# An encoder layer on one core: where the row factors' diagonal is kept, how the turns of two preparing tasks are spaced, and how much dense work stands between the steps of two mLSTMs

## The chip, the cores and the metric

The kernel runs on one core of one Trainium2 chip. The metric is the device time in microseconds (us) of one execution. The kernel before takes 2711.15 us, the median of 3 runs (2709.81 to 2713.0). Engines are named as in the profile: PE is TensorE's matmul, PEld its weight load, DVE is VectorE, ACT ScalarE, POOL GpSimd and SP SyncE, whose queue issues nearly all transfers.

## What is computed

One layer is applied to two sequences, s = 0 with 1024 tokens and s = 1 with 2048, both with 16 learned meta tokens ahead of them. Cut to what matters:

```
xn   = rmsnorm(h) * g_pre
proj = xn @ w_in + b_in                       # 1024 -> 6672 columns, in ten parts
ya   = (neighbourhood_attention(na_q, na_k, na_v) * silu(na_z)) @ w_a
yb   = (mlstm_both_directions(ml_qk, ml_v, ml_g, ml_o) * silu(ml_z)) @ w_b
y    = (sigmoid(ga) * ya + sigmoid(gb) * yb) @ w_out
out  = h + rmsnorm(y) * g_post                # the meta tokens are dropped
```

The mLSTM has 4 heads of 128 columns and works in chunks. Everything is float32; a dense product is made of three matmuls on parts of the operands (high times high, high times low, low times high).

## The kernel before

The work is one **dense** stream and one **sparse** stream, both Python generators. The dense stream (`dense`, `group`, `fm_half`, `tm_unit`, `sgates`, `final`) holds the big products: the projection of blocks of 1024 tokens by groups of columns in the order of `PLAN`, then the output products. The sparse stream (`sparse`) is, in this order, the mLSTM of s = 0 (the short one), the attention of s = 0, the mLSTM of s = 1 (the long one) and the attention of s = 1. A sparse step begins only when the dense columns that it reads are done.

`run` (L2077) weaves the two. A sparse generator yields a number after each step, and `run` then advances the dense stream until as much dense work, in the generators' own estimate (`C512` = 0.235 for a matmul of 512 columns), has been emitted. The numbers are written at the top: `A_D` = 1.63 for a step of an mLSTM's states, `A_A` = 1.79 for a step of its outputs, `A_G` = 1.3 for its gates. PE's instructions stay in the order in which they are emitted. Those of DVE, ACT and of SP's queue are ordered by a scheduler from its own estimates, so a load or a small operation can stand far ahead of the place where the code has it; each engine then works through its list strictly in order, and so does SP's queue.

An mLSTM (`ml`, L1431) runs `ml_states` and then `ml_outputs` for each of 4 heads. `ml_states` has three steps for each chunk of 256 tokens: DVE makes `kf` (L1500), PE transposes it (L1536), and products with the weighted values follow (L202 to L204 into `sm`). The loads of a chunk (`raw`, L1414, and `va`, L1473) are emitted about one chunk ahead. `ml_outputs` has six steps for a block of 256 tokens; its products with `q` and `kh` (L1665, L1666) are the scores.

`build_half` (L466) makes the normalised input of 512 tokens for the dense stream, in steps that are spread among its matmuls. For the four halves of s = 1 it loads four tiles of token rows (`xr`, L398), squares them (L355), computes the four row factors by Newton steps (L161 to L166), and `rdiag` (L362) writes the diagonal matrices of the factors (L367 on ACT, L369 on DVE). `rrows` (L372) multiplies ones with that diagonal on PE (L375), so that each row factor stands in every partition, and copies the product into `rx` (L376). The transposed input comes in four loads (`xt`, L405) into the same ring of four buffers as the token rows, tag `xr`. DVE multiplies each of them by gain and row factors (L524), and ACT and DVE split them into high and low parts (L531, L532). The diagonal is written into the last token tile, so that buffer is free for a load only after PE has read the diagonal, and the fourth `xt` load is emitted behind `rrows`.

The **output ring** is a ring of four buffers named `st` of 528 columns, in which `fm_evac` (L669) puts each finished projection unit before its store (two buffers for a unit of a gated column).

Three **side tasks** are advanced from `beside` (L547), one step in every so many turns of the dense stream: `tprep` (L626) forms sums and differences of the two halves of a 1024-token block for a product scheme with fewer multiplications and stores them (L629, L661, L665; for s = 0 also a copy of the scaled input, L648 to L651), `nprep` and `wprep` (L565) do the like for weights, from which the operands named `q6..` to `q13..` come (L569, L595).

Of the kernel before, what the change touches and what calls it, by code (L numbers as in the profile page):

```python
# [10 lines left out]
F32 = mybir.dt.float32  # L11
# [7 lines left out]
P = 128  # L19
# [112 lines left out]

NBW = 4
C512, C256 = 0.235, 0.12
A_N, A_D, A_A, A_G = (1.08, 0.93), 1.63, 1.79, 1.3


class K:
# [327 lines left out]
    def build_half(self, s, t0, res):  # L466

        nc, wp = self.nc, self.wp
        if (s, t0) in self.xkept:
            assert not self.xput  # L470
            yield
            yield "scaled"
            x = []
            for name, part in zip(("xh", "xl"), self.xkept[s, t0]):
                x.append(wp.tile([P, KT, HALF], F32R, name=name, bufs=2))
                for k in range(0, KT, 4):
                    nc.sync.dma_start(x[-1][:, k:k + 4, :512].bitcast(F32), part[:, k:k + 4, :])
                yield
            res.append(tuple(x))
            return  # L480
        if s == 0:
            xts = self.xnext
            self.xnext = None
            while self.rwait:
                yield "wait"
            self.early = False
            yield "scaled"
            g = self.gpre
            p = self.psum("sm", [P, 512])
            nc.tensor.matmul(p[:, :KT], self.ident, g, start=True, stop=True)  # L490
            g = self.cp.tile([P, KT], F32, name="gx")
            nc.vector.tensor_copy(g, p[:, :KT])
            x, r = self.xparts(), []
            for e in range(4):
                self.xsplit(x, xts[e], e, 0, g)
                self.wflush(2)
                yield
            res.append(tuple(x))
            yield from self.rsum(self.toks, r)
            nc.vector.tensor_copy(self.rc[:, 4:8], r[0])  # L500
            dg = self.rdiag(r[0], self.toks[0][0])

            def rows():
                self.rrows(dg, self.rr[:, 1], "sm")
                self.xp.close()
                self.wside = self.wprep()
                self.sides.append([self.wside, 3])
            self.rwait[s, t0] = rows
        else:
            bp = self.bp  # L510
            toks, r = self.tokens(s, t0, range(4), bp, 4), []
            yield
            yield from self.rsum(toks, r)
            dg = self.rdiag(r[0], toks[3][0])
            xts = [self.xtload(s, t0, e, bp, 4) for e in range(3)]
            yield
            rr = bp.tile([P, 512], F32, name="rx", tag="thT", bufs=1)
            self.rrows(dg, rr, "pj")
            self.loose = False
            xts.append(self.xtload(s, t0, 3, bp, 4))  # L520
            yield
            for k in range(KT):
                v = xts[k // 2][:, k % 2]
                nc.vector.scalar_tensor_tensor(v, v, self.gpre[:, k:k + 1], rr, op0=ALU.mult, op1=ALU.mult)  # L524
                if k % 2:
                    yield
            yield "scaled"
            x = self.xparts()
            for e in range(4):
                h = x[0][:, 2 * e:2 * e + 2, :512]  # L530
                nc.scalar.activation(h, xts[e], AF.Copy)  # L531
                nc.vector.tensor_tensor(x[1][:, 2 * e:2 * e + 2, :512], xts[e], h.bitcast(F32), op=ALU.subtract)  # L532
                yield
            res.append(tuple(x))
            self.loose = True
            self.xkeep(s, t0, x)
# [28 lines left out]
    def wprep(self):  # L565

        nc = self.nc
        unit = {k: j for j, k in enumerate(_weight_units())}
        sub = lambda o, a, b: nc.vector.tensor_tensor(o, a, b, op=ALU.subtract)  # L569
        self.pq = ExitStack()  # L570
        pool = self.pq.enter_context(self.tc.tile_pool(name="pq", bufs=1, side="right", reuse_waits="tile"))
        for p in range(6, 14):
            if p == 10:
                [x for x in self.sides if x[0] is self.wside][0][1] = 4
            raw = pool.tile([P, 2, 2, 512], F32, name="pr", bufs=1)
            for f in range(2):
                nc.sync.dma_start(raw[:, f].rearrange("p a c -> p (a c)"), self.i["wu"][unit["i", PAIRS[p][f], P], :, :D])
            for _ in range(3):
                yield
            for f, ops in ((0, ("11", "12")), (1, ("21", "22")), (1, ("s3", "s1")), (0, ("s2", "s4"))):  # L580
                if ops[0] == "s3":
                    nc.vector.tensor_tensor(raw[:, 1, 1], raw[:, 1, 0], raw[:, 1, 1], op=ALU.add)
                    sub(raw[:, 1, 0], raw[:, 0, 0], raw[:, 1, 0])
                    yield
                if ops[0] == "s2":
                    sub(raw[:, 0, 0], raw[:, 1, 1], raw[:, 0, 0])
                    sub(raw[:, 0, 1], raw[:, 0, 1], raw[:, 0, 0])
                    yield
                o = pool.tile([P, 2, 2, 512], F32R, name="po", bufs=1)
                c = slice(p > 7 and ops[0] == "21", 2)  # L590
                nc.scalar.activation(o[:, c, 0], raw[:, f, c], AF.Copy)
                sub(o[:, c, 1], raw[:, f, c], o[:, c, 0].bitcast(F32))
                for q, op in list(enumerate(ops))[c]:
                    d = self.qd[p, op] = self.dp.tile([P, D], F32, name=f"q{p}{op}")
                    nc.sync.dma_start(d[:, :], o[:, q].rearrange("p a c -> p (a c)").bitcast(F32))  # L595
                yield
                yield

    def nprep(self):

# [25 lines left out]
    def tprep(self, s, t0, after):  # L626
# [11 lines left out]
        for e in range(4):  # L638
# [7 lines left out]
            if s == 0:  # L646
                for a, r in enumerate((r0, r1)):
                    nc.scalar.activation(hi.bitcast(F32R), r, AF.Copy)  # L648
                    tt(ta.bitcast(F32R), r, hi)
                    for d, x in zip(self.xkept[s, t0 + 512 * a], (hi, ta)):  # L650
                        nc.sync.dma_start(d[:, ks, :], x)  # L651
                    yield
            tt(ta[:, 0], r1[:, 0], r0[:, 0])
            tt(ta[:, 1], r1[:, 1], ta[:, 0])
# [362 lines left out]
    def group(self, s, t0, meta, cols, reuse, nxt):  # L1017
# [4 lines left out]
        sw = (s, t0) in SW  # L1022
        if sw and not reuse:
            self.tside = chain(self.tprep(s, t0, 34 if s == 0 else 300 if t0 == 0 else 0), self.nprep() if t0 else ())
            self.sides.append([self.tside, 4 if s == 0 else 2 if t0 else 3])
        for j, (kind, c) in enumerate(jobs):
            if kind == "tm":
                for cost in self.tm_unit(c[0], [(x,) + h for x, h in zip(self.xs, todo)], c[1]):
# [401 lines left out]

    def ml(self, s):  # L1431
        tc, nc = self.tc, self.nc
        T = SEQLEN[s]
        NB = T // BL
        with tc.tile_pool(name=f"mg{s}", bufs=1, side="right", reuse_waits="tile") as keep:
            with tc.tile_pool(name=f"mt{s}", bufs=1, side="right", reuse_waits="tile") as mp:
# [6 lines left out]
            with tc.tile_pool(name=f"ml{s}", bufs=1, side="right", reuse_waits="tile") as mp:  # L1443
# [19 lines left out]
                while norms:  # L1463
                    step()
                    step()
                    yield A_A
        self.done.add(("ml", s))

    def vload(self, mp, s, h, tok, np_, nch):
        nc = self.nc  # L1470
# [604 lines left out]
                yield from self.na(s, rts)  # L2075

    def run(self, ctx):  # L2077
        self.done = set()
        self.setup(ctx)
        dense, acc = self.dense(ctx), 0.0  # L2080
        sparse, start = self.sparse(), 0
        while (w := next(sparse, None)) is not None:
            self.mark(start)
            if isinstance(w, tuple):
# [1 line left out]
                    assert next(dense) is not True  # L2086
                start = len(self.nc.cur_bb.bb.instructions)
                continue
            acc += w
            while acc > 0.0:  # L2090
                d = next(dense, None)
                if d is None or d is True:
# [67 lines left out]
```

## Time and profile before

| what | value |
|---|---|
| median of 3 runs | 2711.15 us |
| the profiled execution, its own time | 2711.91 us |
| its span, first to last instruction | 2710.1 us |
| PE busy | 2647.9 us (98%) |
| DVE busy | 1942.4 us (72%) |
| ACT busy | 1439.5 us (53%) |
| busy share of the 16 DMA engines, by tenths of the slices | 7 to 9 throughout |
| mean granted TensorE clock | 0.991 of full |

The profiled execution took 1.8 us more than its span and 0.8 us more than the median. Times in views are microseconds from the start of the span. A row of a view of windows gives, for each engine, the busy time in that stretch with the number of instructions in brackets; the last three columns are the granted clock, the DMA share and GB/s. The stages, as the trace shows them: the short mLSTM from about 262 to 730 us, the attention of s = 0 to about 1080 us, the long mLSTM from about 1165 to 1940 us, and the attention of s = 1 with the output products to the end.

### The profile page before, as it was taken

What the parts mean: (1) busy time and instruction counts of PE and PEld (TensorE: products, weight loads), DVE (VectorE), ACT (ScalarE), POOL (GpSimd) and SP (SyncE); (2) the same over time, 40 slices, a digit from 0 to 9 for tenths busy, and PEclk for the clock granted to TensorE, in tenths of its full rate; (3) what the DMA queues carried; (4) which work ended last, traced back from release to release, by engine and by line L of the source; (5) the groups of instructions that cost most, each with busy time, mean ns of one, the idle gap of its engine ahead of it and who ended that gap; (6) DMA issues with size and microseconds to landing.
All of it is one profiled execution on the core that took longest, in us unless ns stands there. A gap on an engine that the chain in (4) does not pass through costs nothing.

```text
span 2710.1 us, 47468 instructions
## 1 busy us (share of the span) xinstructions
PE 2647.9 (98%) x15928; PEld 2337.7 (86%) x15928; DVE 1942.4 (72%) x5266; ACT 1439.5 (53%) x3388; POOL 16.4 (1%) x100
## 2 busy tenths in 40 slices
PE   9999898999999999999999999999999999999998
PEld 7998797889987899878888888888889898989888
DVE  5755687879747978536766767757478889897954
ACT  5423555564445655446655566556365665656521
POOL 0000000000000000000000000000000000000000
PEclk9999999999999999999999999999999999999999
DMA  9888976699997899798889998899899798898975
GB/s 367 337 326 337 332 270 224 250 357 353 345 295 229 300 330 303 263 309 266 262 283 294 364 317 257 275 315 392 265 311 304 260 310 260 292 300 271 323 241 204
DMA packets 411652, 805.75 MB, mean 297 GB/s; under 512 B 52017, under 2 KB 180993, under 8 KB 409105
## 3 DMA queue, kind: packets, MB, share of 16 engines
q1 hardware_dynamic: 410288, 800.04, 87.6%
q0 software_dynamic: 1120, 2.69, 0.4%
q8 instruction: 126, 2.06, 0.3%
q14 instruction: 118, 0.96, 0.1%
HBM read 548.96 MB, written 253.60 MB: 296 GB/s over the span
## 4 chain that ended last, share of the span: by engine, by line
PE 72%; DMA 5%; DVE 5%; ACT 1%; issue 1%; SPq 0%; DVEq 0%; ACTq 0%
PE pj L969 7%; PE pj L971 7%; PE pj L970 7%; PE pj L202 6%; PE pj L203 6%; PE pj L204 6%; PE pj L1915 3%; PE pj L1917 3%; PE pj L1916 3%; PE pj L774 3%; PE pj L775 3%; PE pj L776 3%; PE sm L1264 3%; PE tr L1249 2%; PE sm L203 1%
## 5 line engine op out<-in xcount | busy, mean ns | idle before, releaser
L202 PE MATMUL pj<-xh,whi 128*128 128x512 f32 (+1 forms) x896 | 345.6, 386 | 2.2 <-ACT whi L303 1.5
L203 PE MATMUL pj<-xl,whi 128*128 128x512 f32 (+1 forms) x896 | 337.9, 377 | 1.7 <-DVE xl L532 1.7
L204 PE MATMUL pj<-xh,wlo 128*128 128x512 f32 (+1 forms) x896 | 337.2, 376 | 2.3 <-DMA wlo<-wl 2.0
L774 PE MATMUL pj<-whi,xh 128*128 128x256 f32 (+1 forms) x1152 | 331.2, 288 | 0.0
L775 PE MATMUL pj<-wlo,xh 128*128 128x256 f32 (+1 forms) x1152 | 326.4, 283 | 2.9 <-DMA wlo<-wl 2.9
L776 PE MATMUL pj<-whi,xl 128*128 128x256 f32 (+1 forms) x1152 | 326.1, 283 | 0.0
L775 PEld LDWEIGHTS pj<-wlo,xh 128*128 128x128 f32 x1152 | 218.6, 190 | 3.3 <-DMA wlo<-wl 3.2
L1915 PE MATMUL pj<-whi,mh 128*128 128x256 f32 x768 | 219.6, 286 | 0.4 <-DMA whi<-wh 0.4
L774 PEld LDWEIGHTS pj<-whi,xh 128*128 128x128 f32 x1152 | 218.7, 190 | 0.2
L776 PEld LDWEIGHTS pj<-whi,xl 128*128 128x128 f32 x1152 | 218.5, 190 | 0.0
L1917 PE MATMUL pj<-whi,mlo 128*128 128x256 f32 x768 | 216.5, 282 | 0.0
L1916 PE MATMUL pj<-wlo,mh 128*128 128x256 f32 x768 | 216.4, 282 | 0.0
L204 PEld LDWEIGHTS pj<-xh,wlo 128*128 128x128 f32 x896 | 170.6, 190 | 34.9 <-DMA wlo<-wl 2.4
L202 PEld LDWEIGHTS pj<-xh,whi 128*128 128x128 f32 x896 | 170.7, 190 | 30.6 <-ACT whi L303 2.3
L203 PEld LDWEIGHTS pj<-xl,whi 128*128 128x128 f32 x896 | 170.8, 191 | 28.9 <-DVE xl L532 2.4
L1251 ACT ACTIVATE pts<-tr 96x384 fp32r<-96x384 f32 (+2 forms) x192 | 103.3, 538 | 102.6 <-PE tr L1249 101.9
L202 PE MATMUL pj<-yh,whi 128*128 128x512 f32 x384 | 154.7, 403 | 0.0
L203 PE MATMUL pj<-yl,whi 128*128 128x512 f32 x384 | 151.6, 395 | 0.8 <-DVE yl L1817 0.8
L204 PE MATMUL pj<-yh,wlo 128*128 128x512 f32 x384 | 151.9, 396 | 0.0
L1915 PEld LDWEIGHTS pj<-whi,mh 128*128 128x128 f32 x768 | 145.3, 189 | 1.4 <-DMA whi<-wh 0.6
L1916 PEld LDWEIGHTS pj<-wlo,mh 128*128 128x128 f32 x768 | 145.4, 189 | 0.8
L1917 PEld LDWEIGHTS pj<-whi,mlo 128*128 128x128 f32 x768 | 145.3, 189 | 0.0
(366 smaller groups left out, 6939.6 us busy)
## 6 DMA issues: line engine op xcount, KB each, us to landing
whi<-wh SPq DMA_DIRECT2D x136, 512.0 KB
wlo<-wl SPq DMA_DIRECT2D x136, 512.0 KB
whi<-q SPq DMA_DIRECT2D x62, 512.0 KB
wlo<-q SPq DMA_DIRECT2D x50, 512.0 KB
wraw<-wu SPq DMA_DIRECT2D x48, 512.0 KB
gt<-st SPq DMA_DIRECT2D x96, 256.0 KB
tg<-gt SPq DMA_DIRECT2D x96, 256.0 KB
wh<-whi SPq DMA_DIRECT2D x36, 512.0 KB
```

The lines of the kernel that those rows point to most:

```text
L202: mm(out, ah, bh, start=start, stop=False)
L203: mm(out, ah, bl, start=False, stop=False)
L204: mm(out, al, bh, start=False, stop=stop)
L774: nc.tensor.matmul(o, xh, wh, start=k == 0, stop=False)
L775: nc.tensor.matmul(o, xh, wl, start=False, stop=False)
L776: nc.tensor.matmul(o, xl, wh, start=False, stop=k == KT - 1)
L969: mm(bank, w[:, 0, k], xh[:, k], start=fresh and k == 0, stop=False, skip_group_check=True)
L970: mm(bank, w[:, 0, k], xl[:, k], start=False, stop=False, skip_group_check=True)
L971: mm(bank, w[:, 1, k], xh[:, k], start=False, stop=k == 3, skip_group_check=True)
L1915: nc.tensor.matmul(o, mh[:, k, xs], wh, start=clear > 0 and k == 0, stop=False)
L1916: nc.tensor.matmul(o, mh[:, k, xs], wl, start=False, stop=False)
L1917: nc.tensor.matmul(o, ml[:, k, xs], wh, start=False, stop=clear < 2 and k == KT - 1)
```

## The change

- `rdiag` of the four halves of s = 1 gets a buffer of the output ring for the diagonal; the fourth `xt` load is emitted with the other three, ahead of `rrows`.
- `tprep` of s = 0 is advanced in every third turn of the dense stream where it was every fourth, and has one more empty step behind each pair of stores of the scaled input.
- `wprep` waits two steps for its weights where it was three, and has one more empty step behind the first of its four stores.
- While a step of an mLSTM is emitted, the dense work behind it is multiplied by 1.15 (short) or by 0.91 (long). The gates of an mLSTM are among these steps.

```
-A_N, A_D, A_A, A_G = (1.08, 0.93), 1.63, 1.79, 1.3
+A_N, A_D, A_A, A_G, A_S = (1.08, 0.93), 1.63, 1.79, 1.3, (1.15, 0.91)
@@ build_half
-            dg = self.rdiag(r[0], toks[3][0])
-            xts = [self.xtload(s, t0, e, bp, 4) for e in range(3)]
+            dg = self.rdiag(r[0], wp.tile([P, HALF], F32, name="st", bufs=4))
+            xts = [self.xtload(s, t0, e, bp, 4) for e in range(4)]
             yield
             rr = bp.tile([P, 512], F32, name="rx", tag="thT", bufs=1)
             self.rrows(dg, rr, "pj")
             self.loose = False
-            xts.append(self.xtload(s, t0, 3, bp, 4))
             yield
@@ wprep
-            for _ in range(3):
-                yield
+            yield
+            yield
...
                 yield
                 yield
+                if ops[0] == "11":
+                    yield
@@ tprep
                     for d, x in zip(self.xkept[s, t0 + 512 * a], (hi, ta)):
                         nc.sync.dma_start(d[:, ks, :], x)
                     yield
+                    yield
@@ group
-            self.sides.append([self.tside, 4 if s == 0 else 2 if t0 else 3])
+            self.sides.append([self.tside, 3 if s == 0 else 2 if t0 else 3])
@@ ml, run
-        T = SEQLEN[s]
+        T, self.seq = SEQLEN[s], s
...
-            acc += w
+            acc += w * A_S[self.seq] if self.seq is not None else w
```

No instruction is added or taken away on PE; the orders change. Three places follow.

**DVE, in the first build of s = 1** (tokens 0 to 511), while the states of the short mLSTM's second head are made. `xt` are the input tiles, `gpre` the gain, `rx` the row factors, `st` in L1567 and L1653 the mLSTM's states. Before, in one piece:

```order
L1628 TENSOR_TENSOR kl_5350<-kf_5302,kh_5349 128x256 [waits DMAHW2_49,PE_49,Activation_49]
L1653 SCALAR_TENSOR_TENSOR st_5137<-st_5137,g_fb0_3165 128x130 [waits Activation_49]
L524 SCALAR_TENSOR_TENSOR xt_5274<-xt_5274,gpre_90,rx_5270 128x512 [waits DMAHW3_49]
L524 SCALAR_TENSOR_TENSOR xt_5274<-xt_5274,gpre_90,rx_5270 128x512
L1653 SCALAR_TENSOR_TENSOR st_5057<-st_5137,g_fb0_3165,st_5057 128x130 [waits DVE_49]
L684 TENSOR_TENSOR pj_5241<-pj_5241,rr_365 128x512 [waits PE_49]
```

And now (lines are numbered one to three apart in the changed file):

```order
L1570 SCALAR_TENSOR_TENSOR st_5154<-st_5152,g_fb1_3191,sm_5160 128x130 [waits DVE_49,Activation_49]
L523 SCALAR_TENSOR_TENSOR xt_5098<-xt_5098,gpre_90,rx_5129 128x512 x2
L1520 SCALAR_TENSOR_TENSOR vwl_5203<-va1_3220,g_wT0_3173,vwh_5202 128x130 [waits DMAHW3_49,Activation_49]
L1503 SCALAR_TENSOR_TENSOR kf_5282<-th_5280,cv_5255 128x256 [waits DMAHW7_49,PE_49]
L694 SCALAR_TENSOR_TENSOR st_5145<-st_5145,st_5147 128x512 [waits Activation_49]
```

The fourth input tile, `xt_5274`, stood first of the four and waited for a transfer; now none of the four waits for one there.

**SP's queue, at the first chunks of the short mLSTM's first head.** `va` and `raw` are its loads, `xr` and `xt` those of the first build, `q70` and `q71` stores of weight parts. Before:

```order
L1473 DMA va0_3182<-mv0_246 128x2x128 [waits DMAHW1_49,DVE_49]
L1414 DMA raw_3327<-mk00_204 128x258 [waits DMAHW2_49,DVE_49]
L398 DMA xr_5093<-x_sample 128x1024 [waits DMAHW3_49]
L1473 DMA va1_3183<-mv0_246 128x2x128 [waits DMAHW4_49,DVE_49]
L1502 DMA kf00_188<-kf_3292 128x256 [waits DMAHW5_49,DVE_49]
L398 DMA xr_5095<-x_sample 128x1024 [waits DMAHW6_49]
L1414 DMA raw_3417<-mk00_204 128x258 [waits DMAHW7_49,DVE_49,Activation_49]
L331 DMA q70_3340<-whi_3336 128x512 [waits DMAHW0_49,Activation_49]
```

Now:

```order
L405 DMA xt_5104<-xt 128x1024 [waits DMAHW6_49,Activation_49]
L331 DMA q70_3309<-whi_3305 128x512 [waits DMAHW7_49,Activation_49]
L331 DMA q71_3310<-whi_3305 128x512 [waits DMAHW0_49]
L331 DMA q70_3309<-wlo_3306 128x512 [waits DMAHW1_49,DVE_49]
L331 DMA q71_3310<-wlo_3306 128x512 [waits DMAHW2_49]
L274 DMA wraw_3315<-wu 128x1024 [waits DMAHW3_49]
L1476 DMA va0_3219<-mv0_246 128x2x128 [waits DMAHW4_49,DVE_49]
L1416 DMA raw_3387<-mk00_204 128x258 [waits DMAHW5_49,DVE_49,Activation_49]
```

The token loads stood among the head's own loads, and three of the `xt` loads came later in the same head. Now all four `xt` loads, `xt_5104` last, stand ahead of the head's second pair of loads.

**PE, at the product of the first build's row factors.** Before:

```order
L203 MATMUL pj_5241<-xl_288,whi_4980 128x512
L204 MATMUL pj_5241<-xh_287,wlo_4981 128x512
L375 MATMUL pj_5271<-xr_5095,ones_70 128x512 [waits DMAHW6_49]
L202 MATMUL pj_5241<-xh_287,whi_4980 128x512
L203 MATMUL pj_5241<-xl_288,whi_4980 128x512
```

Now, at the same place of the dense stream but for one chunk of the mLSTM:

```order
L203 MATMUL pj_5074<-xl_288,whi_4852 128x512
L204 MATMUL pj_5074<-xh_287,wlo_4853 128x512
L375 MATMUL pj_5130<-st_5093,ones_70 128x512 [waits DVE_49,Activation_49]
L202 MATMUL pj_5074<-xh_287,whi_4852 128x512
L203 MATMUL pj_5074<-xl_288,whi_4852 128x512
```

It reads the ring's buffer and waits for DVE and ACT, where it read the token tile and waited for a transfer.

By the order, there now stand 48 to 56 dense matmuls of 512 columns between the scores of two blocks of the short mLSTM, where there were 42 to 48, and 24 or 25 between two chunks of its states, where there were 18 to 25. In the long one it is 36 to 42 after 42 to 48, and mostly 18 after 18 to 24. The short mLSTM ends later in the dense stream by some 60 us of matmul time, so the third and the fourth build, which fell into the gap between it and the attention of s = 0 and into that attention's first units, now fall into its last outputs and into the gap. The attention of s = 1 begins at the same place of the dense stream.

More of the change, by code (lines that the diff above doesn't have):

```diff
@@ L1467, in ml @@
         self.done.add(("ml", s))
+        self.seq = None
     def vload(self, mp, s, h, tok, np_, nch):
@@ L2077, in run @@
     def run(self, ctx):
-        self.done = set()
+        self.done, self.seq = set(), None
         self.setup(ctx)
```

## The prediction

> **What bounds the kernel now.** I first read the page's top, for the busy engines and for what kernel it is.
>
> ```profile
> span 2710.1 us, 47468 instructions
> PE 2647.9 (98%) x15928; PEld 2337.7 (86%) x15928; DVE 1942.4 (72%) x5266; ACT 1439.5 (53%) x3388; POOL 16.4 (1%) x100
> ```
>
> PE works 98% of the span and the change leaves its instructions as they are. So only two things can give time: PE's idle time, 2710.1 - 2647.9 = 62 us, and the time in which it works at a lower granted clock. Where they lie, a view of windows shows, cut at the places where PE stands still (PE busy, PEld, DVE, ACT, POOL, clock, DMA share, GB/s).
>
> ```profile
> 202.00:262.00 60.00, 59.23 (x339) 51.87 (x338) 34.38 (x48) 19.76 (x28) 0.00 (x0) 1.00 0.92 340
> 294.00:335.00 41.00, 28.63 (x195) 27.12 (x194) 25.17 (x75) 23.04 (x60) 1.91 (x10) 0.88 0.99 370
> 462.00:480.00 18.00, 7.46 (x28) 6.20 (x27) 13.71 (x27) 12.10 (x26) 0.10 (x1) 0.62 0.99 349
> 516.00:523.00 7.00, 5.34 (x26) 4.01 (x25) 7.00 (x15) 2.33 (x4) 0.00 (x0) 1.00 0.40 132
> 676.00:692.00 16.00, 11.14 (x63) 10.45 (x62) 11.49 (x25) 7.70 (x19) 0.10 (x1) 0.68 1.02 379
> 809.00:821.00 12.00, 8.53 (x36) 6.46 (x34) 7.27 (x29) 6.83 (x15) 0.00 (x0) 0.86 1.03 364
> 1164.00:1187.00 23.00, 20.61 (x86) 15.64 (x86) 5.30 (x16) 6.97 (x15) 0.00 (x0) 0.93 0.98 331
> 1187.00:1541.00 354.00, 354.00 (x1764) 295.52 (x1764) 237.32 (x781) 213.38 (x563) 1.00 (x8) 1.00 0.90 290
> 1569.00:1941.00 372.00, 372.00 (x1853) 311.02 (x1852) 250.20 (x838) 212.53 (x557) 3.08 (x14) 1.00 0.91 303
> 1941.00:2705.00 764.00, 752.62 (x4854) 679.61 (x4852) 596.67 (x1514) 406.41 (x981) 2.04 (x4) 1.00 0.87 281
> ```
>
> Six of these windows, from 294:335 to 1164:1187 and 117 us together, in the short mLSTM and near it, hold 12.37 + 10.54 + 1.66 + 4.86 + 3.47 + 2.39 = 35.3 us of PE's idle time, and the low clocks. The two stretches of the long mLSTM hold none. What is behind 1941 us keeps its dense order, and I leave its 11.4 us as they are.
>
> The price of the clock comes from shorter windows behind those gaps.
>
> ```profile
> 298.50:302.50 4.00, 4.00 (x19) 3.69 (x19) 3.04 (x6) 1.94 (x3) 0.00 (x0) 0.57 0.78 237
> 318.40:322.60 4.20, 4.17 (x19) 4.17 (x20) 3.26 (x17) 1.93 (x6) 0.10 (x1) 0.50 1.05 393
> 474.00:479.80 5.80, 5.47 (x19) 4.92 (x20) 4.11 (x11) 3.47 (x10) 0.10 (x1) 0.51 0.99 392
> ```
>
> In 474 to 479.8 us PE, busy at clock 0.51, did in 5.47 us what takes 2.8 at full clock: 2.7 us lost. Elsewhere I take the loss as the window's length times one less its clock, cut down to the busy part: 3.8 us for 294 to 335, 3.0 for 676 to 692, 1.7 for 809 to 821, 1.6 for 1164 to 1187. So what the change can reach is 35.3 idle + 12.8 of clock, some 48 us.
>
> **The first build (462 to 480 us).** The waits of PE, the chain of this stretch and its timeline name one story.
>
> ```profile
> PE tr L1536 <- DVE kf L1500: 11.5, 3, 5.9
> PE sc L1665 <- DVE q L1619: 10.5, 1, 10.5
> 443.40 6.91 DMA xt<-xt
> 450.33 1.42 DVE xt L524 x2
> 454.86 3.98 DVE xt L524 x6
> 460.87 4.20 DMA xr<-x_sample
> 473.76 0.44 DVE q L1619
> 474.33 0.55 PE sc L1665
> 322.25 0.48 DVE L369 TENSOR_SCALAR xr<-ident,nwy 128x128 f32<-128x128 f32 x2
> 439.76 1.02 PE L375 MATMUL pj<-xr,ones 128*128 128x512 f32 x2
> 450.33 1.42 DVE L524 SCALAR_TENSOR_TENSOR xt<-xt,gpre,rx 128x512 f32<-128x512 f32 x2 [5.71 <-DMA xt<-xt]
> ```
>
> The diagonal was ready at 322 us, but it lay in the fourth token buffer, and PE read it only at 439.76. Only then could the fourth input tile be loaded: issued at 443.40, landed 6.91 later. DVE's list has this tile first, so DVE stood idle 5.71 us, and behind it stood the eight multiplications (5.4 us), the splits and, last, `q` (L1619), for which PE's scores waited: 10.54 us idle and 2.7 of clock, 13.2 together. With the diagonal in the ring the order has all four loads some hundred us before L524. The 5.71 us go, and with the backlog in front of `q` (a block of the short mLSTM also has 48 to 56 dense matmuls as cover where it had 42 to 48, at 0.235 us each by the kernel's own estimate 1.4 us more; the 1764 PE instructions in the 354 us above, shorter ones among them, took 0.20 each) the gap should nearly close. It is not certain: the chain also has the next token load, 4.20 us, and ACT's squares, which stay. Bounds: -13.2 if all closes, -6 if only DVE's 5.71 come back. I take **-12**: 5.71 + 1.4 from these, 2.7 of clock, and 2 of the 4.20 for the token load, about half, since buffers come free sooner.
>
> **The first head's states (294 to 335 us).** PE waited three times for `kf`, 11.5 us, and lost 3.8 of clock: 16.2 with the smaller waits.
>
> ```profile
> 307.36 0.37 SPq L1473 DMA_DIRECT2D va<-mv  x1
> 308.04 0.69 SPq L1414 DMA_DIRECT2D raw<-mk  x1
> 317.95 0.43 DVE L1500 SCALAR_TENSOR_TENSOR kf<-th,cv 128x256 f32<-128x256 f32 x1
> ```
>
> The chunk's loads were issued at 308 us, its `kf` made at 317.95. Between them lie landing, ACT and DVE, while the DMA share is 0.99: four token loads and three `xt` loads of 512 KB each run beside them. Now the token loads stand ahead of the head and a chunk has 24 or 25 dense matmuls where it had 18 to 25, up to 7 x 0.23 = 1.6 us more cover per chunk. But four `xt` loads, 2 MB, stand in SP's queue directly ahead of the second chunk's `va` and `raw`; at the window's 370 GB/s that is 5.7 us. Over four chunks the cover could give 6, the early token loads as much again, and the four tiles can take 5.7 back. Bounds -14 and +6; I take **-6**, nearer to the cover, since that is sure.
>
> **The builds 3 and 4, the gap between the stages, the rest.** The waits of DVE at L524 are long here, too.
>
> ```profile
>   ACT rx L376: 15.4, 2
>   DMA xt<-xt: 9.9, 2
> PE pj L775 <- DMA wlo<-wl: 2.9, 1, 2.9
> PE pj L204 <- DMA wlo<-wl: 2.0, 1, 2.0
> ```
>
> At 809 to 821 us (3.47 idle + 1.7 clock) a weight load was late amid the fourth build's loads, at DMA share 1.03. That build's four loads now come earlier, and the build falls to the end of the gap; I take **-3** of 5.2 (bounds -5, +2). At 676 to 692 (4.86 + 3.0 = 7.9) it was a weight load again, in the change from the last outputs to the gap, at share 1.02. The short mLSTM now ends some 60 us later, so other loads meet there, but the third build comes to lie just before: bounds -7 and +5, I take **-2**. At 1164 to 1187 (4.0), the start of the long mLSTM, its gates have 0.91 of the dense work, but they come at other places; **-1**, bounds -4 and +3. The 1.66 at 516 us: the first build's aftermath; **-1**.
>
> **The long mLSTM.** It has 36 to 42 matmuls per block after 42 to 48, and 18 per chunk after up to 24. The slack of a chunk:
>
> ```profile
> 1402.05 0.43 DVE L1500 SCALAR_TENSOR_TENSOR kf<-th,cv 128x256 f32<-128x256 f32 x1 [0.97 <-PE tr L1536]
> 1406.77 0.38 PE L1536 MATMUL tr<-ident,kf 128*128 128x128 f32 x2
> ```
>
> `kf` is ready at 1402.48 and read at 1406.77: 4.3 us. Six matmuls less take at most 1.4. DVE is busy 237 of 354 us, 67%; with a tenth less dense work per step it would be at about 73%. So I expect no steady stall, but single ones where builds, loads and stores meet: **+3**, bounds 0 and +10.
>
> **The sums' turns and `wprep`.** Both run ahead of 262 us. In the 60 us before it PE stands still for 60 - 59.23 = 0.77 us; DVE is busy 34 of the 60 us and ACT 20, so the dense work hides them. If a store in a new place delayed a weight load it would cost as much as the 2.0 or 2.9 above. I take 0 (bounds -0.8, +3).
>
> **What is new.** Four times `rdiag` takes a buffer of the ring in which PE's finished units wait for stores. DVE and ACT, strictly in order, wait there until a buffer is stored; behind them stand `kf`, `vwl` or `q`. One store of 512 columns is 256 KB; I have no row of a wait for it. From the 4.20 and 6.91 us that two loads of 512 KB took, half the size is 2 to 3.5 us, and PE may wait for a part of it, or, with a buffer held for a hundred us, `fm_evac` cycles with three: bounds 0 and +13 (the price of the old stall), I take **+4** with the third build among the outputs, a place in which no build stood.
>
> The sum: -12 - 6 - 3 - 2 - 1 - 1 + 3 + 0 + 4 = **-18**. The profiled execution's own time is 2711.9 (span 2710.1 + 1.8), so 2693.9; the median lies 0.8 below the profiled one, so **2693**.
>
> A rule of the Trainium skill bears on the clock terms, and the sum doesn't rest on it. The trace: of the three waits for `kf`, 11.5 us with the longest 5.9, the two short ones are 2.8 each. The first was followed by clock 0.57 (298.5 to 302.5 us), the last, at 331 us, by full clock, and the wait of 2.0 us for a weight load at 815 us by 0.66:
>
> ```profile
> 331.00:334.00 3.00, 0.19 (x3) 0.01 (x2) 1.59 (x6) 1.74 (x7) 0.00 (x0) 1.00 1.04 374
> 334.00:338.00 4.00, 4.00 (x33) 4.00 (x34) 2.94 (x8) 1.70 (x6) 0.56 (x3) 1.00 0.99 329
> 816.00:821.00 5.00, 3.69 (x11) 2.94 (x12) 0.83 (x3) 1.52 (x4) 0.00 (x0) 0.66 1.04 287
> ```
>
> "TensorE: Matmul & The Clock Gate", section "Why this matters for your kernels", asks for no PE-idle gaps over about 3 us, since one idle window brings the clock back to half. By that, closing gaps under 3 us gives no clock back, and the sum would be about -15, the clock's part of the terms at 676, 809 and 1164 us left out; by the rows a gap under 3 us can cost clock, and it is -18. The trace doesn't agree with the figure as a sharp limit.
>
> **Rivals.** (1) *The transfers bind.* In 294 to 335, 676 to 692 and 809 to 821 us the DMA share is 0.99 to 1.03. If landing times and not the order make these waits, only the first build's 12 come, and the 4 and the 3 of new stalls stay: 2711.2 - 12 - 1 + 7 = 2705, or 2698 without new ones; I say 2702. For it: the full shares. Against: the first build's wait is a matter of order, and the token loads leave the fullest stretch. (2) *The long mLSTM becomes bound by its own chain* (the other side). A block has 36 to 42 matmuls less up to 6 = 1.4 us of cover for 32 blocks, and a chunk up to 1.4 for 36. Its block takes at least 36 x 0.23 = 8.3 us of dense work and its own products; it decides where DVE and ACT need longer for a block than that. If on half of the blocks and chunks the step is 1 us short, that is 34 us more, less the 25 gained before: 2711 + 9 = 2720, from 2710 to 2740. Against: DVE would be at 73%, and 4.3 us of slack. (3) *The ring takes the place of the token buffer*: PE's L375 now waits for DVE and ACT, and one build of four stalls as the old did (+13): 2693 + 9 = 2702 with the +4 counted already; if two do, 2715. (4) *The spacing of sums does nothing*: true by the rows, and the forecast has it at 0.
>
> **How the numbers follow.** Forecast (2693, from 2680 to 2705 with the bounds of its large terms) 0.55; transfers bind (2702) 0.18; the ring (2702, up to 2715) 0.12; the long mLSTM (2720) 0.15. About 5.4 us, 0.2%, is what a measurement of this kernel can tell from no change: faster means under 2705.7, slower over 2716.6. Faster takes 0.50 of the forecast, 0.13 of the transfers, 0.07 of the ring, 0.02 of the last: 0.72. Slower takes 0.09 of the long mLSTM, 0.02 of the ring and 0.01 of the transfers: 0.12. The rest, 0.16, lies within. For 8 in 10 the range goes from 2674, where the first head's states and the builds stand at their good ends, to 2716, which leaves out 0.12 above and some hundredths below.
>
> **What would show it.** Right: no DVE idle over 1 us before the first L523 for a transfer, and PE's wait for L1619 gone; `kf` in the first head with under 6 us of waits; PE 100% through the long mLSTM; L375 with PE idle under 1 us. Wrong: PE waiting for `kf` or `kh` all along 1190 to 1940 us (rival 2), DVE or ACT waiting at `rdiag` for a store (rival 3), waits for weight loads at share 1 (rival 1).

## The result, and the profile after

The changed kernel takes 2709.91 us (median of 12 runs, 2702.43 to 2717.22) where the kernel before, measured in turn with it, takes 2711.64 (12 runs, 2702.86 to 2715.48). The ratio is 0.9998 with a 95% interval from 0.9983 to 1.0012: no change that can be told. 18 us less were forecast, and no change had a chance of 0.16. A second measurement gave 1.0008 (0.9998 to 1.0019). The profiled execution took 2707.9 us.

The page of the changed kernel, its span and the busy engines:

```profile
span 2706.1 us, 47482 instructions
PE 2647.0 (98%) x15928; PEld 2336.6 (86%) x15928; DVE 1943.8 (72%) x5266; ACT 1439.9 (53%) x3388; POOL 16.2 (1%) x100
```

PE's idle time was 2710.1 - 2647.9 = 62.2 us and is 2706.1 - 2647.0 = 59.1. The sum hardly moved, its places did. The windows of the changed kernel (columns as in the prediction):

```profile
202.00:262.00 60.00, 60.00 (x344) 52.68 (x343) 33.58 (x47) 19.92 (x29) 0.00 (x0) 1.00 0.90 328
294.00:335.00 41.00, 29.34 (x207) 28.83 (x206) 22.49 (x65) 18.65 (x46) 1.70 (x10) 0.83 0.84 302
441.00:480.00 39.00, 37.17 (x176) 30.12 (x175) 33.52 (x83) 26.67 (x64) 0.35 (x3) 1.00 0.76 279
620.00:650.00 30.00, 19.51 (x138) 19.01 (x137) 14.27 (x39) 11.16 (x26) 0.00 (x0) 0.77 1.01 351
650.00:700.00 50.00, 50.00 (x428) 50.00 (x427) 45.34 (x148) 21.48 (x56) 0.10 (x1) 1.00 0.92 316
700.00:760.00 60.00, 54.86 (x424) 52.69 (x423) 37.93 (x105) 26.50 (x66) 0.10 (x1) 0.97 0.94 324
760.00:821.00 61.00, 57.98 (x265) 47.51 (x266) 37.26 (x129) 27.87 (x61) 2.48 (x8) 0.95 0.73 246
1164.00:1187.00 23.00, 23.00 (x118) 19.34 (x117) 14.22 (x35) 13.89 (x30) 0.00 (x0) 1.00 0.91 290
1187.00:1541.00 354.00, 351.79 (x1749) 291.83 (x1748) 231.05 (x751) 209.13 (x547) 1.74 (x20) 1.00 0.89 289
1569.00:1941.00 372.00, 368.92 (x1849) 307.98 (x1848) 262.71 (x895) 219.14 (x581) 3.08 (x14) 1.00 0.91 300
```

The same windows of the kernel before, where the prediction had cut them in another way:

```profile
441.00:480.00 39.00, 27.63 (x117) 22.30 (x116) 27.49 (x53) 21.83 (x45) 0.30 (x2) 0.82 0.60 208
620.00:650.00 30.00, 30.00 (x250) 30.00 (x249) 26.80 (x91) 15.84 (x39) 0.10 (x1) 1.00 1.01 355
650.00:700.00 50.00, 45.14 (x349) 44.24 (x348) 39.35 (x94) 18.81 (x48) 0.10 (x1) 0.90 1.02 363
700.00:760.00 60.00, 59.34 (x506) 59.16 (x505) 47.18 (x154) 26.86 (x66) 2.48 (x8) 1.00 0.98 326
760.00:821.00 61.00, 57.52 (x271) 46.99 (x270) 28.00 (x75) 28.81 (x52) 0.00 (x0) 0.97 0.90 295
```

Length less PE's busy time is the idle time. The first build's stall is gone (441 to 480 us: 11.4 idle, now 1.8). The first head's states did not gain (12.4, now 11.7). A new stall of 10.5 us, with clock 0.77, stands at 620 to 650 us where PE never stopped, and 700 to 760 us went from 0.7 to 5.1, while 650 to 700 fell from 4.9 to 0. The two stretches of the long mLSTM have 2.2 + 3.1 where they had none; the 28 us between them, which no row above shows, had 2.8 and have 1.4. The waits of PE name the two large ones.

```profile
PE tr L1539 <- DVE kf L1503: 11.7, 2, 8.9
PE pj L776 <- DMA whi<-wh: 6.8, 1, 6.8
```

The timeline shows how they come about; the number in brackets is the idle time ahead of an instruction, with what ended it.

```profile
278.07 0.44 SPq L398 DMA_DIRECT2D xr<-x_sample  x1
281.08 1.97 SPq L398 DMA_DIRECT2D xr<-x_sample  x3
290.78 0.32 SPq L1416 DMA_DIRECT2D raw<-mk  x1
...
298.51 1.05 ACT L355 ACTIVATE xsq<-xr 128x1024 bf16<-128x1024 f32 x1
299.89 0.17 DVE L161 TENSOR_SCALAR nwy<-ss 128x4 int32<-128x4 int32 x1
301.87 0.16 DVE L166 SCALAR_TENSOR_TENSOR nwy<-nwt,nwy 128x4 f32<-128x4 f32 x1
303.19 0.48 DVE L1428 SCALAR_TENSOR_TENSOR cv<-raw,cw,cv 128x256 f32<-128x256 f32 x1
307.23 0.42 DVE L1503 SCALAR_TENSOR_TENSOR kf<-th,cv 128x256 f32<-128x256 f32 x1
307.71 0.69 PE L1539 MATMUL tr<-ident,kf 128*128 128x128 f32 x2 [8.86 <-DVE kf L1503]
...
626.60 1.45 SPq L576 DMA_DIRECT2D pr<-wu  x2
630.63 0.32 SPq L667 DMA_DIRECT2D t3h<-xr  x1
631.03 0.47 SPq L296 DMA_DIRECT2D whi<-wh  x1
635.84 0.46 SPq L296 DMA_DIRECT2D wlo<-wl  x1
637.75 0.58 PE L776 MATMUL pj<-whi,xh 128*128 128x256 f32 x1 [6.83 <-DMA whi<-wh]
642.00 0.58 PE L777 MATMUL pj<-wlo,xh 128*128 128x256 f32 x1 [3.66 <-DMA wlo<-wl]
```

In the first head all four token loads of the first build stand ahead of the head's own `raw`, and its fourth square and Newton steps (L161 to L166) stand in ACT's and DVE's lists ahead of the first chunk's `cv`; `kf` is made at 307.23 us, PE was free at 298.85. The chunk's own load isn't what is late: in the trace its packets end at 296.5 us, and ACT first reads them (L1425) at 300.50. The fourth square and the Newton steps fill 3.5 us, from 298.51 to 302.03, and splits of weights (L303, L304, L568) stand between them and `kf` as well. At 631 us a unit's weights were issued only when PE needed them. The same matmul (the 3361st on a `pj` tile) starts at 652.89 us in the kernel before, whose loads were issued 14 and 8 us ahead:

```profile
638.63 0.32 SPq L296 DMA_DIRECT2D whi<-wh  x1
645.17 0.49 SPq L296 DMA_DIRECT2D wlo<-wl  x1
652.89 0.36 PE L774 MATMUL pj<-whi,xh 128*128 128x256 f32 x1
```

With more dense work per step the dense stream is there 15 to 22 us sooner. SP's queue, behind sums (`t3h`), weights for the pairs (`pr`) and the mLSTM's loads, is only 7.6 us sooner with the first of the two loads.

### The profile page after: what moved, and what is told of

The parts are those of the page before. It is cut to its first block, busy times and chain, and to the rows that moved or that the text cites. A ratio compares the mean times of both kernels' runs of the same rounds, so it can differ in the third digit from the quotient of the medians.

```text
span 2706.1 us, 47482 instructions
## 1 busy us (share of the span) xinstructions
PE 2647.0 (98%) x15928; PEld 2336.6 (86%) x15928; DVE 1943.8 (72%) x5266; ACT 1439.9 (53%) x3388; POOL 16.2 (1%) x100
## 4 chain that ended last, share of the span: by engine, by line
PE 82%; DMA 9%; DVE 5%; ACT 2%; issue 1%; SPq 1%; DVEq 0%; ACTq 0%
PE pj L202 9%; PE pj L204 9%; PE pj L203 9%; PE pj L971 7%; PE pj L973 7%; PE pj L972 7%; PE pj L776 4%; PE pj L777 4%; PE pj L778 4%; PE pj L1918 3%; PE pj L1919 3%; PE pj L1920 3%; PE sm L1266 3%; PE tr L1251 2%; DMA wraw<-wu 2%
## 5 line engine op out<-in xcount | busy, mean ns | idle before, releaser
L1258 DVE TENSOR_TENSOR pts<-tr,pts 96x384 fp32r<-96x384 f32 (+2 forms) x192 | 118.5, 617 | 57.2 <-ACT pts L1253 55.3
```

## The experiments

Each was measured in five rounds beside the kernel before, whose median there was 2710.2 to 2711.4 us; a changed kernel has 4 to 12 executions. "Idle and clock" in the expectations is PE's idle time and, added to it, half of its busy time at the lower granted clock. A line number shifts by a few between kernels.

### Is a stall the property of an order?

**The changed kernel again, unedited.**

> The changed kernel unchanged, to see which of its stalls come back in a second profiled execution. If the stalls belong to the order: kf at 299 us 8 to 10 us and the two weight loads at 631 us 9 to 12 us again, each within 2 us. If they belong to the moment (how the transfers fall in one execution): other places, or sizes more than 4 us off.

Ratio 1.0008 (0.9998 to 1.0019). `kf` at 298.85 us waited 8.85 us (8.86 before), the two weight loads 5.6 and 3.6 us:

```profile
PE pj L776 <- DMA whi<-wh: 5.6, 1, 5.6
```

So these stalls belong to the order, and profiles of single executions can be compared at them, though whole times spread by 0.5%. Not every wait comes back: at 700 to 760 us PE waited 3.4 us for a weight load that it had not waited for in the first profile, and the window's idle time was 8.5 us after 5.1. So 3 us in one window of waits for transfers is what two profiles of one kernel can differ by.

### One part alone, one part undone

**The ring alone:**

```diff
-            dg = self.rdiag(r[0], toks[3][0])
-            xts = [self.xtload(s, t0, e, bp, 4) for e in range(3)]
+            dg = self.rdiag(r[0], wp.tile([P, HALF], F32, name="st", bufs=4))
+            xts = [self.xtload(s, t0, e, bp, 4) for e in range(4)]
...
-            xts.append(self.xtload(s, t0, 3, bp, 4))
```

> The kernel before with the ring's diagonal alone. Theory 1 (each stall is an accident of one order: the first build's is gone for good): PE's wait for q in the first build, 10.54 us before, is under 2, PE's idle time from 262 to 821 us falls from 35.5 to about 25, time -12 us against before. Theory 2 (the transfers bind: idle time in the short mLSTM moves and doesn't go): the wait for q is gone too, but waits for weight loads or kf elsewhere from 262 to 821 us bring the idle time there to 32 or more, time within 5 us of before.

Ratio 1.0003 (0.9992 to 1.0015). Neither expectation holds in full: the stall is neither gone nor moved far. In 441 to 480 us the idle time falls from 11.4 to 7.1, and 480 to 523 us rises from 1.7 to 3.5; with the clock, the two come to 14.9 us after 15.7. A row of its waits and one of its timeline:

```profile
PE sc L1664 <- DVE q L1618: 4.1, 1, 4.1
```

```profile
444.12 1.13 PE L375 MATMUL pj<-st,ones 128*128 128x512 f32 x2 [3.00 <-ACT st L367]
```

The load no longer makes DVE wait, but the diagonal is now written at 443 us, just ahead of its product, and PE waits 3.0 us for it; the eight multiplications and the splits still stand ahead of `q`.

**The multipliers alone:**

```diff
-A_N, A_D, A_A, A_G = (1.08, 0.93), 1.63, 1.79, 1.3
+A_N, A_D, A_A, A_G, A_S = (1.08, 0.93), 1.63, 1.79, 1.3, (1.15, 0.91)
...
-            acc += w
+            acc += w * A_S[self.seq] if self.seq is not None else w
```

> The kernel before with the multipliers 1.15 and 0.91 alone, diagonal and spacing as before. Theory 1: the multipliers make the new stalls of the changed kernel (kf at 299 us, 8.9 us; two weight loads at 631 us, 10.5 us) and the old one of the first build stays: idle from 262 to 821 us some 45 us, time +10 to +20 us. Theory 2: idle stays at 30 to 38, time within 5 us of before.

Ratio 0.9978 (0.9966 to 0.9990), some 5 to 6 us faster than before. Theory 1 missed the sign, and theory 2 the idle time (28.6 us from 262 to 821 us): the first build's stall goes without the ring.

```profile
294.00:335.00 41.00, 34.67 (x251) 33.33 (x250) 25.00 (x73) 23.68 (x61) 2.14 (x10) 0.92 1.01 358
441.00:480.00 39.00, 36.22 (x167) 28.92 (x165) 30.46 (x79) 27.25 (x62) 0.41 (x3) 1.00 0.90 338
620.00:650.00 30.00, 20.68 (x159) 20.18 (x158) 16.31 (x52) 10.38 (x26) 0.00 (x0) 0.83 1.04 358
...
429.23 0.33 SPq L405 DMA_DIRECT2D xt<-xt  x1
433.33 1.40 DVE L524 SCALAR_TENSOR_TENSOR xt<-xt,gpre,rx 128x512 f32<-128x512 f32 x2
```

Idle is 6.3 us in the first head (12.4 before), 2.8 in the first build (11.4), and 9.3 at the weight loads (0). The last two rows are of its timeline and show how the build's stall went: the diagonal still lies in the token tile, but the fourth tile's load is issued at 429.23 us (443.40 before), and the eight multiplications run in three pieces from 433.33 to 441.0, between steps of the head, where they ran from 450.33 to 458.8. Ahead of them DVE waits 0.2 us for `rx` (L376) and not at all for the load, for which it waited 5.71. The multiplier of the short mLSTM thus makes by itself both the gain and the stall at 631 us, and not the one at 299 us.

**The changed kernel without multipliers** (A_S at 1.0 and 1.0).

> The changed kernel with the multipliers at 1 and 1: ring and spacing stay. Theory 1: neither the first build's stall nor those at 299 and 631 us, idle from 262 to 821 us 20 to 25, time -10 us against before. Theory 2: idle 30 to 38, within 5 us of before.

Ratio 1.0005 (0.9994 to 1.0016). As theory 2 has it in time and in the sum: 31.8 us idle from 262 to 821 us, among it 11.5 for `kf` at 295 and 313 us, 4.4 for `q` in the first build and 6.1 for `kh` at 673. The stall at 631 us is not there, as theory 1 has it.

**The changed kernel with the diagonal in the token tile** (the first diff the other way round), and **with the old spacing** of `tprep` and `wprep`:

```diff
-            self.sides.append([self.tside, 3 if s == 0 else 2 if t0 else 3])
+            self.sides.append([self.tside, 4 if s == 0 else 2 if t0 else 3])
```

and without the empty steps more and fewer.

> The changed kernel with the diagonal back in the fourth token tile: multipliers and spacing stay. Theory A (the ring brings the stall for kf at 299 us, since the four input loads and their squares crowd the first head's start): no gap over 3 us at 299, 294 to 335 us costs 7 to 9 us of idle and clock as with the multipliers alone, time 0.2% under before. Theory B (the spacing of the sums brings it): 15 to 17 us there again, time as the changed kernel's. In both the first build has no gap over 3 us, because the cover comes from the multiplier, and the two weight loads near 628 us cost 9 to 11 us again.

> The changed kernel with the old spacing of tprep and wprep: ring and multipliers stay. Theory A (the ring brings the stall at 299 us): 15 to 17 us of idle and clock from 294 to 335 us, time as before within 0.2%. Theory B (the spacing brings it): 7 to 9 us there, time 0.2% under before.

With the old diagonal 1.0003 (0.9992 to 1.0013), with the old spacing 0.9973 (0.9961 to 0.9984). Theory B: the spacing brings the stall. The timeline of the kernel with the old spacing:

```profile
275.61 0.32 SPq L664 DMA_DIRECT2D t0h<-xr  x1
286.03 1.58 SPq L398 DMA_DIRECT2D xr<-x_sample  x3
287.66 0.70 SPq L1413 DMA_DIRECT2D raw<-mk  x1
298.40 0.47 DVE L1425 SCALAR_TENSOR_TENSOR cv<-raw,cw,cv 128x256 f32<-128x256 f32 x1
300.79 0.42 DVE L1500 SCALAR_TENSOR_TENSOR kf<-th,cv 128x256 f32<-128x256 f32 x1
301.98 0.27 PE L1536 MATMUL tr<-ident,kf 128*128 128x128 f32 x1
307.91 0.42 SPq L398 DMA_DIRECT2D xr<-x_sample  x1
```

`kf` is made at 300.79 us and PE doesn't wait; one wait of 6.7 us, at 316 us, is left. The sums are stored from 275.61 on (`t0h`; from 260.58 in the changed kernel), out of tiles named `xr`, and only three token loads come ahead of the head. The fourth comes at 307.91, so the four factors are computed behind the first chunk.

### Which edit of the spacing

**tprep's edits alone, wprep's alone** (each beside ring and multipliers), then **of tprep only the turns, only the empty step**:

```diff
-            self.sides.append([self.tside, 4 if s == 0 else 2 if t0 else 3])
+            self.sides.append([self.tside, 3 if s == 0 else 2 if t0 else 3])
```

```diff
                     for d, x in zip(self.xkept[s, t0 + 512 * a], (hi, ta)):
                         nc.sync.dma_start(d[:, ks, :], x)
                     yield
+                    yield
```

> The changed kernel with wprep's waits as before: ring, multipliers and tprep's turns (every third, one more empty step) stay. If tprep's turns bring the stall for kf at 299 us: its gap is over 7 us, 15 to 17 us of idle and clock from 294 to 335 us, time as before within 0.2%. If wprep's waits bring it: 7 to 9 us there, time 0.2% to 0.3% under before, as with the old spacing.

> The changed kernel with tprep's turns as before: ring, multipliers and wprep's waits stay. If tprep's turns bring the stall at 299 us: 7 to 9 us of idle and clock from 294 to 335 us, time 0.2% to 0.3% under before. If wprep's waits bring it: 15 to 17 us, time as before. If it takes both: 7 to 9 us in this kernel and in the one with tprep's turns alone.

> Ring and multipliers as in the changed kernel, wprep as before, and of tprep only the turns (every third for every fourth, no empty step more). If the stall at 299 us comes from tprep's earlier end, which frees the token buffers so that all four loads, squares and Newton steps of the first build stand ahead of the first head: a gap over 7 us for the first kf, 15 to 17 us of idle and clock from 294 to 335 us. If it comes from the empty step: 7 to 9 us there.

> Ring and multipliers as in the changed kernel, wprep as before, and of tprep only the one more empty step (every fourth turn stays). If the stall at 299 us comes from tprep's earlier end: no gap over 3 us at the first kf, under 10 us of idle and clock from 294 to 335 us, time 0.1% to 0.3% under before. If it comes from the empty step: 15 to 17 us.

Ratios: `tprep`'s edits 0.9984 (0.9974 to 0.9994), `wprep`'s 0.9960 (0.9948 to 0.9972), turns 0.9985 (0.9975 to 0.9994), step 0.9967 (0.9954 to 0.9980). The waits for `kf`, of the kernel with the turns:

```profile
PE tr L1536 <- DVE kf L1500: 9.6, 2, 7.5
```

and the window of the first head in the kernel with the step:

```profile
294.00:335.00 41.00, 37.87 (x261) 35.95 (x259) 28.25 (x70) 21.68 (x54) 1.83 (x9) 0.92 0.97 338
```

The turns bring a gap of 7.5 us at 301 us, the step none there: 3.1 us idle in the whole window, and its token loads come only from 326 us on. All five kernels that have the turns and the multiplier 1.15 show a gap of 7.5 to 10.6 us at 298 to 301 us; the eight with 1.15 and without the turns show none there, but most of them one of 5.4 to 6.8 us at 315 us; with the turns one of 2.1 to 2.8 us follows, at 324. In all, the window has 9.6 to 13.4 us of idle time with the turns and 3.1 to 6.8 without. That the squares and Newton steps are what stands in between is read from the lists and the timeline; no kernel moved them alone. In idle and clock the turns alone came to 11.0 us in that window, not the 15 to 17 expected. In whole times `tprep`'s edits cost 3 us beside the old `wprep` (0.9984 against 0.9973, and the intervals meet) and 10 us beside the new one (0.9998 against 0.9960, and they don't). `wprep`'s edits gave less time without `tprep`'s (0.9960 against 0.9973, the intervals meet) and more with them: 0.9998 and 1.0008 against 0.9984, where the first interval meets and the second doesn't. Why the two add up so stays open: in the first head the kernels with and without `wprep`'s edits have the same 11.7 us of idle time.

### The multipliers are a pair

**1.15 and 1.0**, then **1.0 and 0.91**, each in the kernel before.

> The kernel before with the multipliers 1.15 and 1.0 alone. If the long mLSTM's 0.91 costs what the trace of the changed kernel shows, idle from 1187 to 1941 us falls from 6.2 (with 0.91) to under 2.5, and the time is 2 to 4 us under that of 1.15 and 0.91 together (2705), some 2702. If 0.91 pays back in the attention of s = 1 behind it (14.1 there, with 1.0 16.6 to 19.7), the two cancel: 2705 within 2.

> The kernel before with the multipliers 1.0 and 0.91 alone. If 0.91 costs only the long mLSTM's cover: the first 1160 us as before, idle from 1187 to 1941 us some 6 us where it was 2.8, time +3 to +6 us. If the two multipliers only pay as a pair, because the long mLSTM must end at the place of the dense stream where the attention of s = 1 can begin: it ends too early, the attention waits for its columns while the dense stream runs alone, and the time is either as before (dense work hides it) or more than 10 us longer.

Ratios 1.0163 (1.0143 to 1.0182) and 1.0064 (1.0052 to 1.0077), 44 and 17 to 19 us slower. The 0.91 that I had down as a cost is what gives the 1.15 its gain. With 1.0 for the long mLSTM the attention of s = 1 begins at 2020 us, behind 9190 matmuls on `pj` tiles, where it is 1958 and 8938 before and 1952 and 8938 with the pair; 564 are left behind its end, where it is 779. It lacks dense work as cover, above all at the end:

```profile
2500.00:2700.00 200.00, 184.54 (x1049) 161.07 (x1050) 146.83 (x358) 87.10 (x213) 0.00 (x0) 0.91 0.75 247
```

15.5 us idle at clock 0.91, where the kernel before has 1.4 at full clock. With 0.91 alone the attention begins at 1914 us, behind 8686 matmuls, and meets a wait of its own:

```profile
PE sc L1217 <- ACT kd L1192: 7.3, 1, 7.3
```

That profiled execution took 2724.1 us, 12 more than the profiled one before: 12 us of idle time are in its trace. Why the median, 2730, is higher by another 6 is open.

### What makes the weight loads late

**1.15 and 1.0, with `wprep` slowed** from its seventh pair on, then **the changed kernel with it**:

```diff
+            if p == 12:
+                [x for x in self.sides if x[0] is self.wside][0][1] = 8
```

> As the multipliers 1.15 and 1.0 alone, with wprep advanced only in every 8th turn from its seventh pair on, so that 4 MB of its stores and loads leave the stretch from 590 to 650 us for later. If the waits for weight loads near 628 us come from transfers that share the queue and the DMA engines: their 9.3 us fall under 4, and the time is 6 to 9 us under that of the kernel without the delay. If they come from the place of the weight loads' own buffers (freed too late by PE): they stay at 8 to 11 us.

> The changed kernel, with wprep advanced only in every 8th turn from its seventh pair on. If its waits for weight loads at 631 us (10.5 us of idle and 3.2 of clock) are made by the transfers beside them: under 2 us from 620 to 650 us, 294 to 335 us as in the changed kernel (16 us), time 5 to 10 us under the changed kernel's 2710 to 2712. If by the weight buffers: 12 to 14 us as before and the same time.

The first has the ratio 1.0158 (1.0139 to 1.0176), 1.0163 without the edit: 2 us less where 6 to 9 were expected. Idle time from 262 to 821 us fell from 29.3 to 23.8, but behind 1941 us, where the unpaired multipliers lack cover, it rose from 39.5 to 44.2. In the changed kernel the edit gives 0.9956 (0.9942 to 0.9969), 13 us under before and 11 to 14 under the changed kernel, more than the 5 to 10 expected. In both PE doesn't stop at 620 to 650 us; the changed kernel with the late pairs:

```profile
294.00:335.00 41.00, 29.34 (x216) 28.92 (x215) 22.42 (x65) 18.65 (x46) 1.70 (x10) 0.83 0.85 305
620.00:650.00 30.00, 30.00 (x255) 30.00 (x255) 27.21 (x85) 15.09 (x40) 0.00 (x0) 1.00 1.01 345
```

The DMA share is 1.01 with the stall and without it, and the rate moves little (351 and 345 GB/s). What changed is the place in SP's queue: the unit's `whi` was issued at 613.82 us, 17 us ahead of where it was, and 16 ahead of its use at 630.21. The edit also takes `wprep`'s own transfers out of the stretch; no run moved the load alone. The Trainium skill ("Perfetto Trace Analysis", section "Identifying the Most-Contended Engine") holds that occupancy misleads with 16 DMA engines. This window agrees: 1.01 before the change, 1.01 with 10.5 us of waiting, 1.01 without.

### Joined

**Old spacing and late pairs**, then **`wprep`'s edits and late pairs** (both with ring and multipliers).

> The changed kernel with the old spacing and wprep advanced only in every 8th turn from its seventh pair on. The waits for weight loads near 628 us (5.3 us of idle and 2.4 of clock with the old spacing) go, others near 740 us grow by some 4 us, as they did with the multipliers 1.15 and 1.0: 2 to 7 us under the kernel with the old spacing (2703.5), so 2697 to 2702, 0.3% to 0.5% under before.

> The changed kernel without tprep's edits, and with wprep advanced only in every 8th turn from its seventh pair on. If both stalls go (299 and 631 us) the time is that of the kernel with the old spacing and the late pairs, 2697, or up to 4 us less: 0.5% to 0.65% under before. If the waits of wprep bring other collisions when it is slowed: 2698 to 2704.

2697.4 us, ratio 0.9946 (0.9933 to 0.9959), and 2693.9 us, ratio 0.9941 (0.9928 to 0.9955): both beat the kernel before and the changed one, the former by 14 and 17 us. Both lie where they were expected, but no wait grew at 740 us: from 700 to 760 us the first has 3.7 us of idle time where the old spacing alone has 4.8. They can't be told from each other.

## Why the prediction was wrong

Two terms didn't come, in idle and clock together. The first head, for which -6 was taken, is where it was (16.2 us, now 16.1). The stretch of the later builds and weight loads, for which -3 and -2 were taken, rose from 14.4 to 26.3 us (620 to 821 us), nearly as much as the first build brought. Behind them two steps of the working failed: the spacing, taken at 0, and the weight loads, priced by the builds' loads alone.

- **The first build, -12 and -1.** The size was right: 441 to 523 us lost 11.2 us of idle time and all of the low clock. The reason was wrong, so the size was luck. The ring, to which I gave most, takes DVE's 5.71 us away but only 2.5 us of PE's idle time, and of what is left 3.0 is a new wait at L375; the multiplier alone takes 10.2. In the changed kernel the diagonal's place makes no difference: 1.8 us are idle there with the ring and with the token tile. The 1.4 us of cover for a block isn't the reason either. With the multiplier the build comes at another place among the mLSTM's steps, and its fourth tile is there in time.
- **The first head, -6.** It moved by 0.7 us of idle time. The multipliers alone gave 6.0, which is the term. I counted the early token loads as a second gain; by the lists, they are what took the first away, since their squares and Newton steps come with them.
- **The sums' turns and `wprep`, 0.** This step failed. I had priced the place ahead of 262 us, where nothing happens (0.77 us idle, now 0), and not what the earlier end of `tprep` sets free: the buffers of the next build's loads. It costs a gap of 7.5 to 10.6 us at 299 us, and 3 to 10 us of the whole time. That both run ahead of 262 us was false, too. In the kernel before, `tprep` of s = 0 stores until 280 us, and `wprep` loads until 636 us and stores until 728:

```profile
L577 SPq DMA_DIRECT2D pr<-wu x16: 382/986/1523, 59.5 to 635.6; - x16
```

- **The builds 3 and 4 and the weight loads, -3 and -2.** This step failed as well, with the sign of the first rival and at a place that I did not price. From 620 to 821 us idle time was 9.0 us and is 18.7. I asked which loads the builds bring, and not that a faster dense stream needs its own weights sooner from a queue that doesn't run faster. That rival, at 2702, was closer in number, and its sign, a wait for weight loads at share 1, came. Its mechanism, landing times and not the order, didn't: with `wprep` slowed the load stands 17 us earlier in the queue, and the wait is gone at the same share.
- **The start of the long mLSTM, -1, and its cover, +3.** 2.4 us of idle time gone and 3.9 come, from 1187 to 1941 us: right in sign and near in size. That 0.91 is needed for the balance, I did not see, though the order before the prediction showed the attention of s = 1 at the same place of the dense stream.
- **New stalls at the ring, +4.** In the changed kernel none: its L375 doesn't wait. With the ring alone it was 3.0 us at the first build.
- **Rivals.** The second, a long mLSTM bound by its own chain, did not come. The third came at a quarter of its price, without the multipliers only. For the first, a share of 7 to 9 tenths throughout, as the table of the kernel before has it, is too high: two of its slices are at 6 and the last at 5, and the first build's stall lay in a stretch of share 0.60.

In sum: the multipliers bring some 5 to 6 us by themselves, the ring adds nothing that can be told, and the spacing takes it back: with ring and multipliers the old spacing has 0.9973, the new one 0.9998 and 1.0008. The largest single stall, the weight loads at 631 us, comes with the multipliers; with `wprep` slowed it is gone, and the changed kernel has 0.9956.

## What to carry to other kernels

When one stream is sped up against another, price what it reads from a queue that is not sped up: take the first need of each load, before and after, against its issue. A task that ends earlier frees buffers, and what was waiting for them moves up in every engine's list; look there, not at the task's own place. Multipliers that hold a meeting place of two streams come as a pair, and each alone can cost several times what the pair brings.

## What was not expected of the hardware

- Twelve executions of the changed kernel spread from 2702.4 to 2717.2 us, 0.5%, while the same gap measured 8.86 us in the profiled one of them and 8.85 us in a profiled one of the second measurement.
- A window at DMA share 1.01 held PE for 10.5 us in one order and for none in two others.
